# A two-layer hybrid decoder trunk: the down projection's second column half by seven products, and a convolution's lags split over two engines

## The chip, the cores and the metric

One core of one Trainium2 chip runs the whole program. The metric is the device time of one execution in microseconds (us). Engines are named as in the profile: PE is TensorE (matmuls), PEld its weight loads, DVE is VectorE, ACT is ScalarE, POOL is GpSimd, and SP is SyncE, which here only issues transfers.

## The reference

Two layers over 256 tokens of width 2048, in float32. Each layer is a mixer with a residual add, a gated feed-forward block with a convolution, and a gated per-layer embedding. Only the feed-forward block is touched:

```python
def causal_dwconv(x, w):                      # width 3, along the tokens
    width, s = w.shape[0], x.shape[1]
    xp = jnp.pad(x, ((0, 0), (width - 1, 0), (0, 0)))
    y = xp[:, 0:s] * w[0]
    for j in range(1, width):
        y = y + xp[:, j:j + s] * w[j]
    return y

def conv_ffn(hn, w_up, conv_w, conv_b, w_down):
    u = causal_dwconv(hn @ w_up, conv_w) + conv_b   # w_up: 2048 x 11264
    gate, up = jnp.split(u, 2, axis=-1)
    return (jax.nn.silu(gate) * up) @ w_down        # w_down: 5632 x 2048
...
h = h + conv_ffn(rmsnorm(h, ffn_norm), w_up, conv_w, conv_b, w_down)
```

## The kernel before

**Split precision.** A float32 operand is cut into a high part (`hi`, a cast on ScalarE, line 188) and a rest (`lo`, a difference on VectorE, line 189), in pieces of 128 x 1024. A product takes three matmuls: high by high, rest by high, high by rest. Four buffers for `hi` and four for `lo` (`WB`) set how far the casts run ahead of TensorE. Weights arrive in four raw buffers of 1 MiB (`RAWB`), loaded through SP's queue.

**The up projection.** `conv` handles 256 channels. `gemm_b` makes them in two units; a unit reads 1 MiB of weights, casts two pieces and issues 16 matmuls of 512 columns (line 267, both parts of the activations side by side) and 16 of 256 (line 272). `joined` adds the two halves of the PSUM result (lines 279, 280) and scales it (line 282). Then come the convolution (line 1072: one tap and the bias on ScalarE; line 1074: the two lags on VectorE), the gate (lines 1083, 1084) and `put_split`, which cuts the result into an activation tile (lines 482, 483). Two tiles of 128 channels of the feed-forward width (44 in all) take two such convolutions, one for the gate and one for the other half.

**The down projection.** `w_down` is worked through in groups of eight tiles, the first of four: (0,4), (4,12), ... (36,44). While one group is made by `up`, the group before it is multiplied by `down`, a unit of one between units of the other. A plain unit (`gemm_a`) takes four tiles by 512 columns for both token halves: 24 matmuls (lines 296, 297, 302).

**Seven products.** For the four groups in the middle, the first 1024 of the 2048 columns are done as a 2 x 2 block product with seven block products and not eight (`seven`). The left factors, sums of the activation blocks, are made by `Forms` (lines 381 to 389). The right factors are sums of weight blocks: a running total in two activation-sized buffers (`xg`), loaded by SP (`put`, line 408) and added to by transfers that POOL issues with an addition (`plus`, line 412), and fresh blocks in raw buffers (`fresh`). One product (`product`, lines 443, 444, 448) has 12 matmuls and casts two pieces. VectorE adds the results into `h` (lines 454 to 479); one sum of two weight blocks is made on VectorE (line 472). The other 1024 columns go by `plain` (line 1100).

**Order.** Each engine runs its queue in order. A scheduler of the framework orders the instructions of each engine when the program is built, from the order of the calls and their dependences. `SHARE` is 0.8: after each up unit 0.8 of a unit of `down` is due. `down` alternates one unit of `plain` with two of `seven`. The up projection runs two units (`LAG`) before the first of them. After the last group, `proj_add` does its down projection plainly (the tail) and feeds the next normalization (lines 316 to 338).

Of the kernel before, what the change touches and what calls it, by code (L numbers as in the profile page):

```python
# [16 lines left out]
AF = mybir.ActivationFunctionType  # L17
# [4 lines left out]
P = 128  # L22
# [11 lines left out]
UNIT = 3  # L34
LAG = 2
SHARE = 0.8
RATES = [1.7, 1.1, 1.1, 0.95, 2.8]
# [48 lines left out]
def trunk(ctx: ExitStack, tc: tile.TileContext, a: dict):  # L86
# [311 lines left out]
    class Quads:  # L398
# [15 lines left out]
        def begin(self):  # L414
            self.put(self.total, 0, 0)
            self.plus(0, 1)

# [8 lines left out]

    def seven(quads, tiles, forms, then):

        c, run_t, fresh, plus = quads.c, quads.total, quads.fresh, quads.plus

# [20 lines left out]
        h11, h12, h21, h22 = h[0][c], h[0][c + 1], h[1][c], h[1][c + 1]  # L451
        one = pb()
        yield from product(one, forms.left(0), run_t, True)
        V.tensor_sub(h22, h22, one)
        V.tensor_sub(h12, h12, one)
        plus(1, 1)
        acc = pb()
        yield from product(acc, x(0, 0), fresh(0, 0), True)
        V.tensor_add(h11, h11, acc)
        one = pb()  # L460
        yield from product(one, x(1, 0), fresh(1, 0), True)
        V.tensor_add(h11, h11, one)
        yield from product(acc, forms.left(1), run_t, False)
        V.tensor_sub(h12, h12, acc)
        plus(1, 0)
        one = pb()
        b22 = fresh(1, 1)
        yield from product(one, forms.left(3), b22, True)
        V.tensor_sub(h12, h12, one)
        t3 = fresh(0, 1)  # L470
        for q in range(2):
            V.tensor_add(t3[q], t3[q], b22[q])
        yield from product(acc, forms.left(2), t3, False)
        V.tensor_sub(h22, h22, acc)
        V.tensor_add(h21, h21, acc)
        one = pb()
        yield from product(one, x(1, 1), run_t, True)
        then()
        V.tensor_add(h21, h21, one)

# [575 lines left out]
    def ffn(l, nf, nxt, aside=None):  # L1056
# [9 lines left out]
        def conv(cb, j0):  # L1066
            ps = yield from gemm_b(w_up, cb, Xf)
            u = joined(ps, nf.bc)
            y = t2((P, 2, S))
            for j in range(2):  # L1070
                ct = j0 + j
                A.activation(y[:, j], u[:, j], AF.Identity, scale=fc(ct + 176), bias=fc(ct + 264))  # L1072
                for lag in range(1, 3):
                    V.scalar_tensor_tensor(y[:, j, lag:], u[:, j, : S - lag], fc(ct + (2 - lag) * 88), y[:, j, lag:], op0=ALU.mult, op1=ALU.add)  # L1074
            return y
# [15 lines left out]

        def down(g0, g1, tiles, forms, quads, then):
            r0, nk = g0 * P, g1 - g0

            def plain(cols):
                for c in cols:
                    ps = [pb() for _ in range(NH)]
                    yield from gemm_a(w_dn, r0, nk, c * 512, 512, tiles, ps)
                    for i in range(NH):
                        V.tensor_add(h[i][c], h[i][c], ps[i])  # L1100

            if forms is None:
                then()
                yield from plain(range(CG))
                return
            fast = seven(quads, tiles, forms, then)
            slow = plain(range(2, CG))
            going = True
            while going:
                going = False  # L1110
                for part in (slow, fast, fast):
                    for _ in range(UNIT):
                        if next(part, part) is not part:
                            going = True
                            yield

        groups = [(max(g - 4, 0), g + 4) for g in range(0, NFT, 8)]
        prev = None
        total = []

        def following(g0):
            if g0 + 8 < NFT:
                if not total:
                    total.extend(running())
                quads.append(Quads(w_dn, g0 * P, 0, total))
                quads[-1].begin()

        quads = []
        for g0, g1 in groups:
            forms = Forms() if 0 < g0 and g1 < NFT else None  # L1130
            cur = (g0, g1, [], forms)
            going = up(g0, g1, cur[2], forms)
            if prev is not None:
                behind_it = down(*prev, quads[-1] if quads else None, partial(following, g0))
                for _ in range(LAG * UNIT):
                    next(going)
                owed = 0.0
                for n, _ in enumerate(going, 1):
                    if n % UNIT:
                        continue  # L1140
                    owed += SHARE
                    if owed >= 1.0:
                        owed -= 1.0
                        for _ in range(UNIT):
                            next(behind_it, None)
                run(behind_it)
            else:
                run(going)
            if g0 == 4 and aside is not None:
                aside()  # L1150
            if g1 + 8 == NFT:
                pin.append(ple_input(l))
# [342 lines left out]
```

## Time and profile before

| | before |
|---|---|
| median of 3 runs | 2880.49 us (2878.83 to 2880.64) |
| profiled execution | 2880.58 us, span 2878.8 us |
| PE busy | 2860.8 us (99%) |
| DVE busy | 2060.9 us (72%) |
| ACT busy | 1537.8 us (53%) |
| transfers | 562.49 MB, mean 195 GB/s |

The span goes from the first to the last instruction of the one execution that the profiler recorded; its own time is 1.8 us longer. Busy times are unions per engine and can overlap between engines. The two feed-forward stages lie at about 500 to 1200 and 2100 to 2725 us of the span.

### The profile page before, as it was taken

How to read it: one execution, taken by the hardware profiler on the slowest of the kernel's cores; microseconds unless marked ns; L12 is line 12 of the kernel's file. 1: busy time of each engine (PE TensorE's matmuls, PEld its weight loads, DVE VectorE, ACT ScalarE, POOL GpSimd, SP SyncE). 2: the span in 40 equal slices, each digit the busy share in tenths (PEclk: the TensorE clock that was granted, in tenths of full speed). 3: DMA queues.
4: the chain of work that ended last, by engine and by line, in shares of the span. 5: the costliest groups of instructions: out<-in, count | busy, mean ns of one | idle time of the engine just before them, and what ended most of it. 6: DMA issues, size and time to landing. Idle time of an engine off the chain costs nothing.

```text
span 2878.8 us, 38652 instructions
## 1 busy us (share of the span) xinstructions
PE 2860.8 (99%) x15076; PEld 2464.2 (86%) x15076; DVE 2060.9 (72%) x2898; ACT 1537.8 (53%) x2185; POOL 121.8 (4%) x116
## 2 busy tenths in 40 slices
PE   9999999999999999999999999999999999999998
PEld 8899988888888888888888888888888888888887
DVE  7888867778878887656556565655668878788765
ACT  7666655555555555554444444344545555555554
POOL 0111100000000000000000000000000000000000
PEclk9999999999999999999999999999999999999999
DMA  7444445757878787555555555555575777877654
GB/s 236 135 132 131 138 161 194 221 189 203 249 206 235 233 232 225 171 183 192 179 185 186 191 181 182 186 179 189 186 222 185 220 232 223 238 220 223 212 185 145
DMA packets 410040, 562.49 MB, mean 195 GB/s; under 512 B 10752, under 2 KB 266880, under 8 KB 409856
## 3 DMA queue, kind: packets, MB, share of 16 engines
q1 hardware_dynamic: 393376, 530.05, 56.2%
q0 software_dynamic: 13056, 25.17, 5.3%
q10 hardware_dynamic: 3424, 4.79, 0.5%
q8 instruction: 118, 1.93, 0.3%
q14 instruction: 66, 0.54, 0.1%
HBM read 557.87 MB, written 2.10 MB: 195 GB/s over the span
## 4 chain that ended last, share of the span: by engine, by line
PE 98%; DVE 1%; ACT 0%; DMA 0%; issue 0%; POOL 0%; ACTq 0%; POOLq 0%; DVEq 0%
PE pa L267 30%; PE pa L272 16%; PE pa L297 10%; PE pa L296 10%; PE pa L302 10%; PE pb L297 3%; PE pb L296 3%; PE pb L302 3%; PE pb L444 2%; PE pb L443 2%; PE pb L448 2%; PE pb L739 2%; PE pb L316 1%; PE pa L936 1%; PE pb L745 0%; PE pb L1234 0%
## 5 line engine op out<-in xcount | busy, mean ns | idle before, releaser
L189 DVE TENSOR_TENSOR lo<-raw,hi 128x1024 fp32r<-128x1024 f32 (+3 forms) x1140 | 1197.9, 1075 | 555.8 <-ACT hi L188 498.8
L188 ACT CAST hi<-raw 128x1024 fp32r<-128x1024 f32 (+3 forms) x1140 | 1010.0, 931 | 955.5 <-PE pa L297 327.6
L267 PE MATMUL pa<-xg,hi 128*128 128x512 f32 x3840 | 925.9, 392 | 0.0
L267 PEld LDWEIGHTS pa<-xg,hi 128*128 128x128 f32 x3840 | 709.7, 188 | 140.6 <-DVE xg L321 0.3
L296 PE MATMUL pa<-hi,xg 128*128 128x512 f32 (+1 forms) x1348 | 522.8, 388 | 2.0 <-ACT hi L188 1.9
L297 PE MATMUL pa<-hi,xg 128*128 128x512 f32 (+1 forms) x1348 | 521.4, 387 | 0.3 <-DVE xg L321 0.2
L272 PEld LDWEIGHTS pa<-xg,lo 128*128 128x128 f32 x3840 | 490.3, 191 | 16.3
L272 PE MATMUL pa<-xg,lo 128*128 128x256 f32 x3840 | 502.0, 283 | 0.0
L302 PE MATMUL pa<-lo,xg 128*128 128x512 f32 (+1 forms) x1348 | 331.7, 386 | 0.0
L296 PEld LDWEIGHTS pa<-hi,xg 128*128 128x128 f32 x1348 | 253.9, 188 | 50.5 <-ACT hi L188 2.2
L297 PEld LDWEIGHTS pa<-hi,xg 128*128 128x128 f32 x1348 | 253.7, 188 | 49.4 <-DVE xg L321 0.8
L302 PEld LDWEIGHTS pa<-lo,xg 128*128 128x128 f32 x1348 | 250.1, 188 | 47.9
L1074 DVE SCALAR_TENSOR_TENSOR t<-t,fp,t 128x255 f32<-128x255 f32 (+1 forms) x352 | 154.0, 479 | 49.8 <-ACT t L1072 48.5
L297 PE MATMUL pb<-hi,xg 128*128 128x512 f32 x348 | 135.9, 391 | 0.0
L296 PE MATMUL pb<-hi,xg 128*128 128x512 f32 x348 | 135.8, 390 | 0.0
L279 ACT COPY t<-pa 128x512 f32<-128x512 f32 x128 | 75.1, 587 | 76.8 <-PE pa L272 67.6
L412 POOL DMA_DIRECT2D xg<-in_l_ffn_w_down_dram x48 | 57.9, 1206 | 1174.5 <-DVE t L1074 419.9
L1072 ACT ACTIVATE t<-t,fp 128x256 f32<-128x256 f32 x176 | 96.1, 593 | 13.4 <-DVE t L282 13.4
L157 POOL TENSOR_TENSOR small<-small,mhalf 128x1 f32<-128x1 f32 (+2 forms) x38 | 28.8, 757 | 1401.1 <-DVE small L1264 622.6
L280 DVE TENSOR_TENSOR t<-t,pa 128x512 f32<-128x512 f32 x128 | 87.1, 680 | 1.1 <-ACT t L279 1.1
L302 PE MATMUL pb<-lo,xg 128*128 128x512 f32 x348 | 86.5, 389 | 0.0
L321 DVE SCALAR_TENSOR_TENSOR xg<-pb,par,xg 128x256 fp32r<-128x256 f32 x136 | 60.0, 479 | 35.8 <-ACT xg L320 35.0
(280 smaller groups left out, 2233.8 us busy)
## 6 DMA issues: line engine op xcount, KB each, us to landing
raw<-in_l_ffn_w_up_dram SPq DMA_DIRECT2D x176, 1024.0 KB, 5.2
raw<-in_l_w_in_dram SPq DMA_DIRECT2D x128, 1024.0 KB, 5.1
raw<-in_l_ffn_w_down_dram SPq DMA_DIRECT2D x56, 1024.0 KB, 5.2
raw<-in_l_w_out_dram SPq DMA_DIRECT2D x44, 1024.0 KB, 5.1
raw<-in_l_ffn_w_down_dram SPq DMA_DIRECT2D x64, 512.0 KB, 4.9
raw<-in_l_ple_gate_dram SPq DMA_DIRECT2D x32, 1024.0 KB, 5.1
xg<-in_l_ffn_w_down_dram POOLq DMA_DIRECT2D x48, 512.0 KB, 6.8
xg<-in_l_ffn_w_down_dram SPq DMA_DIRECT2D x16, 512.0 KB, 4.6
```

The costliest lines, as they stand in the source:

```text
L188: last_cast[0] = A.copy(vo(hi)[:, c], vi(rk)[:, c])
L189: last_diff[0] = V.tensor_sub(vo(lo)[:, c], vi(rk)[:, c], vo(hi)[:, c].bitcast(F32))
L267: last_mm[0] = T.matmul(ps[:, j], wh, x2, start=first, stop=False)
L272: last_mm[0] = T.matmul(ps[:, j, :S], lo[k][:, j * P : (j + 1) * P], xr(tiles, c * 8 + k)[1], start=False, stop=c == 1 and k == 7)
L279: A.copy(u, ps[:, :, S:])
L280: V.tensor_add(u, u, ps[:, :, :S])
L296: T.matmul(o[i], xh, hi[k], start=begin and k0 + k == 0, stop=False)
L297: last_mm[0] = T.matmul(o[i], xw, hi[k], start=False, stop=False)
L302: last_mm[0] = T.matmul(o[i], xl(tiles, k0 + k, i)[0], lo[k], start=False, stop=end and k0 + k == nkb - 1)
L321: V.scalar_tensor_tensor(t[:, kk, 1], pk, g, t[:, kk, 0].bitcast(F32), op0=ALU.mult, op1=ALU.subtract)
L1072: A.activation(y[:, j], u[:, j], AF.Identity, scale=fc(ct + 176), bias=fc(ct + 264))
L1074: V.scalar_tensor_tensor(y[:, j, lag:], u[:, j, : S - lag], fc(ct + (2 - lag) * 88), y[:, j, lag:], op0=ALU.mult, op1=ALU.add)
```

## The change

The groups start at tile 0 and have eight tiles: (0,8), (8,16), ... (32,40), and the last has four, (40,44). `by_seven` says which column halves of a group go by seven products: both for the first four groups, the first half for (32,40). The last group is plain, as the tail. With both halves by seven, `down` has two `seven` one after the other and no plain part; the units due after each up unit follow from the count of units (1.0 there, 11/6 in the last group).

Within `seven` the order of the products changes. The running total starts as the block B11 alone (one load) and is used for the first product as it is; the block B12 is added afterwards. Before, B11 was loaded a second time, fresh. Products now add on in the same PSUM bank after VectorE has read it, so that seven additions into `h` are left of nine. At the end, `then` loads the total for the next half.

The two lags of the convolution were four operations on VectorE for 256 channels (multiply and add, 254 or 255 elements). They become four scaled copies on ScalarE (256 elements each) and two additions on VectorE over both channel blocks.

```diff
--- before.py
+++ after.py
@@ -33,7 +33,6 @@
 PSB = 4
 UNIT = 3
 LAG = 2
-SHARE = 0.8
 RATES = [1.7, 1.1, 1.1, 0.95, 2.8]
 D = 2048
 S = 256
@@ -413,7 +412,6 @@
 
         def begin(self):
             self.put(self.total, 0, 0)
-            self.plus(0, 1)
 
         def fresh(self, hh, e):
             raw = rawp.tile([P, 4, 512], F32, tag="raw", name=nm("raw"))
@@ -424,8 +422,9 @@
     def running():
         return [xtile().bitcast(F32).rearrange("p a b c -> p a (b c)") for _ in range(2)]
 
-    def seven(quads, tiles, forms, then):
-
+    def seven(ready, tiles, forms, then):
+
+        quads = ready.popleft()
         c, run_t, fresh, plus = quads.c, quads.total, quads.fresh, quads.plus
 
         def x(half, i):
@@ -449,34 +448,31 @@
             yield
 
         h11, h12, h21, h22 = h[0][c], h[0][c + 1], h[1][c], h[1][c + 1]
-        one = pb()
-        yield from product(one, forms.left(0), run_t, True)
-        V.tensor_sub(h22, h22, one)
-        V.tensor_sub(h12, h12, one)
-        plus(1, 1)
         acc = pb()
-        yield from product(acc, x(0, 0), fresh(0, 0), True)
+        yield from product(acc, x(0, 0), run_t, True)
         V.tensor_add(h11, h11, acc)
+        plus(0, 1)
         one = pb()
         yield from product(one, x(1, 0), fresh(1, 0), True)
         V.tensor_add(h11, h11, one)
+        two = pb()
+        yield from product(two, forms.left(0), run_t, True)
+        V.tensor_sub(h22, h22, two)
+        plus(1, 1)
+        b22 = fresh(1, 1)
+        yield from product(two, forms.left(3), b22, False)
+        V.tensor_sub(h12, h12, two)
+        t3 = fresh(0, 1)
+        for q in range(2):
+            V.tensor_add(t3[q], t3[q], b22[q])
         yield from product(acc, forms.left(1), run_t, False)
         V.tensor_sub(h12, h12, acc)
         plus(1, 0)
-        one = pb()
-        b22 = fresh(1, 1)
-        yield from product(one, forms.left(3), b22, True)
-        V.tensor_sub(h12, h12, one)
-        t3 = fresh(0, 1)
-        for q in range(2):
-            V.tensor_add(t3[q], t3[q], b22[q])
         yield from product(acc, forms.left(2), t3, False)
         V.tensor_sub(h22, h22, acc)
+        yield from product(acc, x(1, 1), run_t, False)
+        then()
         V.tensor_add(h21, h21, acc)
-        one = pb()
-        yield from product(one, x(1, 1), run_t, True)
-        then()
-        V.tensor_add(h21, h21, one)
 
     def put_split(t, k, n, src):
         A.copy(t[:, k : k + n, 0], src)
@@ -1070,8 +1066,11 @@
             for j in range(2):
                 ct = j0 + j
                 A.activation(y[:, j], u[:, j], AF.Identity, scale=fc(ct + 176), bias=fc(ct + 264))
-                for lag in range(1, 3):
-                    V.scalar_tensor_tensor(y[:, j, lag:], u[:, j, : S - lag], fc(ct + (2 - lag) * 88), y[:, j, lag:], op0=ALU.mult, op1=ALU.add)
+            for lag in range(1, 3):
+                z = t2((P, 2, S))
+                for j in range(2):
+                    A.activation(z[:, j], u[:, j], AF.Copy, scale=fc(j0 + j + (2 - lag) * 88))
+                V.tensor_add(y[:, :, lag:], y[:, :, lag:], z[:, :, : S - lag])
             return y
 
         def up(g0, g1, tiles, forms):
@@ -1089,66 +1088,68 @@
                         forms.add(*kept)
                         kept = []
 
-        def down(g0, g1, tiles, forms, quads, then):
-            r0, nk = g0 * P, g1 - g0
-
-            def plain(cols):
-                for c in cols:
-                    ps = [pb() for _ in range(NH)]
-                    yield from gemm_a(w_dn, r0, nk, c * 512, 512, tiles, ps)
-                    for i in range(NH):
-                        V.tensor_add(h[i][c], h[i][c], ps[i])
-
-            if forms is None:
-                then()
-                yield from plain(range(CG))
-                return
-            fast = seven(quads, tiles, forms, then)
-            slow = plain(range(2, CG))
+        def plain(g0, g1, tiles, cols):
+            for c in cols:
+                ps = [pb() for _ in range(NH)]
+                yield from gemm_a(w_dn, g0 * P, g1 - g0, c * 512, 512, tiles, ps)
+                for i in range(NH):
+                    V.tensor_add(h[i][c], h[i][c], ps[i])
+
+        groups = [(g, min(g + 8, NFT)) for g in range(0, NFT, 8)]
+        by_seven = {g0: [0, 2] if n < len(groups) - 2 else [0] for n, (g0, g1) in enumerate(groups[:-1])}
+        jobs = deque((g0, c) for g0, cols in by_seven.items() for c in cols)
+        ready = deque()
+        total = []
+
+        def following():
+            if not total:
+                total.extend(running())
+            if jobs:
+                g0, c = jobs.popleft()
+                ready.append(Quads(w_dn, g0 * P, c, total))
+                ready[-1].begin()
+
+        def down(g0, g1, tiles, forms):
+            fast = chain(*[seven(ready, tiles, forms, following) for _ in by_seven[g0]])
+            rest = [c for c in range(CG) if c - c % 2 not in by_seven[g0]]
+            slow = plain(g0, g1, tiles, rest)
+            parts = [slow, fast, fast] if rest else [fast]
             going = True
             while going:
                 going = False
-                for part in (slow, fast, fast):
+                for part in parts:
                     for _ in range(UNIT):
                         if next(part, part) is not part:
                             going = True
                             yield
 
-        groups = [(max(g - 4, 0), g + 4) for g in range(0, NFT, 8)]
         prev = None
-        total = []
-
-        def following(g0):
-            if g0 + 8 < NFT:
-                if not total:
-                    total.extend(running())
-                quads.append(Quads(w_dn, g0 * P, 0, total))
-                quads[-1].begin()
-
-        quads = []
-        for g0, g1 in groups:
-            forms = Forms() if 0 < g0 and g1 < NFT else None
+        for n, (g0, g1) in enumerate(groups):
+            forms = Forms() if g1 < NFT else None
             cur = (g0, g1, [], forms)
             going = up(g0, g1, cur[2], forms)
-            if prev is not None:
-                behind_it = down(*prev, quads[-1] if quads else None, partial(following, g0))
-                for _ in range(LAG * UNIT):
-                    next(going)
+            for _ in range(LAG * UNIT):
+                next(going)
+            if prev is None:
+                following()
+                run(going)
+            else:
+                behind_it = down(*prev)
+                share = sum(7 if c in by_seven[prev[0]] else 2 for c in range(0, CG, 2)) + 2 * (len(by_seven[prev[0]]) == 1)
+                share /= 2 * (g1 - g0) - LAG
                 owed = 0.0
-                for n, _ in enumerate(going, 1):
-                    if n % UNIT:
+                for m, _ in enumerate(going, 1):
+                    if m % UNIT:
                         continue
-                    owed += SHARE
-                    if owed >= 1.0:
+                    owed += share
+                    while owed >= 1.0:
                         owed -= 1.0
                         for _ in range(UNIT):
                             next(behind_it, None)
                 run(behind_it)
-            else:
-                run(going)
-            if g0 == 4 and aside is not None:
+            if n == 1 and aside is not None:
                 aside()
-            if g1 + 8 == NFT:
+            if n == len(groups) - 2:
                 pin.append(ple_input(l))
             prev = cur
         later(lambda: pin.append(ple_tiles(pin.pop())))
```

## Rows read from the trace of the kernel before

**Rows 1.** The page: busy us of each engine; the chain that ended last, by engine.

```profile
PE 2860.8 (99%) x15076; PEld 2464.2 (86%) x15076; DVE 2060.9 (72%) x2898; ACT 1537.8 (53%) x2185; POOL 121.8 (4%) x116
...
PE 98%; DVE 1%; ACT 0%; DMA 0%; issue 0%; POOL 0%; ACTq 0%; POOLq 0%; DVEq 0%
```

**Rows 2.** Windows: stretch, length, busy us (instructions) by engine, clock, DMA share, GB/s.

```profile
500.00:1200.00 700.00, 700.00 (x3734) 605.43 (x3733) 556.21 (x735) 392.51 (x496) 29.00 (x24) 1.00 0.72 218
2100.00:2725.00 625.00, 625.00 (x3349) 542.07 (x3348) 497.43 (x647) 349.82 (x430) 28.91 (x24) 1.00 0.73 220
890.55:1020.41 129.86, 129.86 (x694) 112.49 (x693) 105.46 (x138) 73.67 (x90) 7.22 (x6) 1.00 0.76 227
```

**Rows 3.** Timeline of PE in that group: start, us, line, operands, count.

```profile
903.23 3.82 PE L267 MATMUL pa<-xg,hi 128*128 128x512 f32 x16
...
906.88 2.08 PE L272 MATMUL pa<-xg,lo 128*128 128x256 f32 x16
...
908.79 3.82 PE L267 MATMUL pa<-xg,hi 128*128 128x512 f32 x16
...
919.93 0.40 PE L296 MATMUL pb<-hi,xg 128*128 128x512 f32 x1
...
925.39 3.79 PE L267 MATMUL pa<-xg,hi 128*128 128x512 f32 x16
...
930.93 0.40 PE L443 MATMUL pb<-hi,t 128*128 128x512 f32 x1
...
933.68 3.79 PE L267 MATMUL pa<-xg,hi 128*128 128x512 f32 x16
```

**Rows 4.** Groups by form, DVE, 890.55 to 1020.41: busy us, mean ns | idle before.

```profile
L189 DVE TENSOR_TENSOR lo<-raw,hi 128x1024 fp32r<-128x1024 f32 x48 | 57.9, 1220 | 14.9 <-ACT hi L188 14.0 <-PE pa L272 0.6 <-issue 0.3
...
L1074 DVE SCALAR_TENSOR_TENSOR t<-t,fp,t 128x255 f32<-128x255 f32 x16 | 7.3, 480 | 3.4 <-ACT t L1072 3.4
L1074 DVE SCALAR_TENSOR_TENSOR t<-t,fp,t 128x254 f32<-128x254 f32 x16 | 7.2, 479 | 0.1
L282 DVE TENSOR_TENSOR t<-t,rbc 128x512 f32<-128x512 f32 x8 | 5.5, 685 | 0.0
...
L1100 DVE TENSOR_TENSOR t<-t,pb 128x512 f32<-128x512 f32 x4 | 2.7, 684 | 5.0 <-PE pb L302 5.0
L472 DVE TENSOR_TENSOR raw<-raw,raw 128x1024 f32<-128x1024 f32 x2 | 2.5, 1226 | 0.1
```

**Rows 5.** Groups by form, ACT, the same stretch.

```profile
L188 ACT CAST hi<-raw 128x1024 fp32r<-128x1024 f32 x48 | 48.4, 1048 | 37.6 <-PE pa L267 19.4 <-issue 9.6 <-PE pb L297 6.0
L1072 ACT ACTIVATE t<-t,fp 128x256 f32<-128x256 f32 x16 | 8.7, 594 | 1.5 <-DVE t L282 1.5
```

**Rows 6.** Line 320, a copy with a scale: ns min/median/max, first and last start.

```profile
L320 ACT ACTIVATE xg<-pb,par x136: 454/467/515, 7.7 to 2775.0; 128x256 fp32r<-128x256 f32 x136
```

**Rows 7.** DMA queues, 890.55 to 1020.41: packets, MB, share of 16 engines.

```profile
q1 hardware_dynamic: 21464, 26.21, 61.2%
q0 software_dynamic: 1632, 3.15, 14.5%
```

**Rows 8.** Timeline around one addition to the running total.

```profile
922.87 1.05 ACT L188 CAST hi<-xg 128x1024 fp32r<-128x1024 f32 x1 [2.16 <-PE pb L297]
...
927.30 1.22 DVE L189 TENSOR_TENSOR lo<-xg,hi 128x1024 fp32r<-128x1024 f32 x1
927.54 2.50 POOL L412 DMA_DIRECT2D xg<-in_l_ffn_w_down_dram  x2 [29.22 <-DVE t L1074]
```

**Rows 9.** The page, DMA issues: count, KB each, median us to landing.

```profile
xg<-in_l_ffn_w_down_dram POOLq DMA_DIRECT2D x48, 512.0 KB, 6.8
xg<-in_l_ffn_w_down_dram SPq DMA_DIRECT2D x16, 512.0 KB, 4.6
```

**Rows 10.** Timeline of ACT at the end of a layer's last up unit.

```profile
1154.87 0.59 ACT L279 COPY t<-pa 128x512 f32<-128x512 f32 x1 [0.82 <-PE pa L272]
...
1163.09 0.63 ACT L482 CAST xg<-t 128x512 fp32r<-128x512 f32 x1 [0.24 <-DVE t L1084]
```

## The prediction

> **What bounds the kernel now.** I read the page first: TensorE is busy for nearly the whole span [rows 1]. That alone proves little, since matmuls overlap in the trace, so the windows over the two feed-forward stages come next. The change lies wholly in these 1,325 us, and there TensorE is busy for 700.00 of 700.00 and 625.00 of 625.00 us, with the clock at 1.00 [rows 2], its upper level of 2.4 GHz. The chain of waits agrees: nothing but matmul lines, one behind the other. So a wait of another engine costs nothing today, and a matmul that goes is worth its distance to the next one.
>
> Third comes the timeline of one group, for that distance. A unit of the up projection starts its 512-column matmuls at 903.23, its 256-column ones at 906.88, and the next unit starts at 908.79: 5.56 us. A plain unit of the down projection (24 matmuls) runs from 919.93 to 925.39: 5.46 us. A product of the seven (12 matmuls) from 930.93 to 933.68: 2.75 us [rows 3]. Check: a group of eight tiles now takes 16 up units, 7 products and 4 plain units, 88.96 + 19.25 + 21.84 = 130.05 us; its period in the trace, from one reload of the running total at 890.55 to the next, is 129.86.
>
> Fourth, the other resources of that group: VectorE is busy 105.46 us of 129.86 (81%), ScalarE 73.67 (57%), the DMA engines 76% [rows 2]. These are the covers that the change spends.
>
> **The change part by part.**
>
> *Fewer matmuls.* Today four groups of a layer do one column half by seven products and one plainly; the rest is plain. Afterwards the five full groups do nine of ten halves by seven. A half costs 4 plain units, 21.84 us, or 7 products, 19.25: 2.59 saved. Five halves more in each of two layers: 10 x 2.59 = 25.9 us. Counted by matmuls it is 12 fewer per half, 120 x 0.228 (3.65/16, [rows 3]) = 27.4; I take 25.9, which contains the joints between units, and 27.4 as the outer bound.
>
> *VectorE.* In a group whose down projection is all seven (four per layer), the 32 lag operations go: 7.3 + 7.2 us. In their place stand 16 additions of 510 or 508 elements. Nearest row: the 512-element addition with both operands in SBUF, 5.5 us for 8, so 11.0. The second half makes 14 casts where the plain one made 8; six more differences at 57.9/48 = 1.21 are 7.2. The sum for one product (b22 into t3) comes twice, +2.5. Additions into h: 7 + 7 instead of 9 + 4, +0.7 [rows 4]. Sum: 105.5 - 14.5 + 11.0 + 7.2 + 2.5 + 0.7 = 112.4 us. The group itself shrinks to 16 x 5.56 + 14 x 2.75 = 127.5. So VectorE goes from 81% to 88%: hidden, with 15 us of slack instead of 24.
>
> *ScalarE.* Per group 32 scaled copies of 256 elements come new. None like them, SBUF to SBUF with a column as scale, is in the trace: below is the copy with such a scale out of PSUM, 0.467 [rows 6], above the activation with scale and bias, 0.594 [rows 5]. That is 15 to 19 us; I take 16, nearer to the copy, since only the scale is read. Six more casts at 48.4/48 = 1.01 add 6. Total 73.7 + 16 + 6 = 96 us of 127.5, 75%: hidden in sum.
>
> *DMA.* Per group the up weights stay 16 MiB. A seven's half drops from 8 to 7 MiB (B11 is now used from the running total and not loaded again), but the plain half of 4 becomes 7; three of each seven are additions into SBUF, on POOL's queue. Today SP's queue takes 61.2% of 129.86 us for 26.21 MB, 3.03 us a MB, and POOL's 14.5% for 3.15 MB, 5.98 [rows 7]. Afterwards 25.2 x 3.03 + 6.3 x 5.98 = 76 + 38 = 114 us, 89% of 127.5. Hidden, but the second cover that becomes thin.
>
> *The running total.* It is cast for products 1, 3, 5 and 7, and an addition lands in between. Products 1 and 3 are now two up units and one product apart, 16.6 us start to start. In the trace, from the first cast of such a product (922.87) the last difference starts at 927.30 and ends at 928.5, and POOL issues two additions from 927.54 [rows 8]. They land after 6.8 us [rows 9]. The first half is thus there 11.5 us and the second about 13 us after the first cast. 3.6 us are left, so I price it at zero; the casts' lead over TensorE (922.87 against 930.93, 8 us) covers it, too.
>
> The reload from the seventh product to the first of the second half is tighter, because only one up unit lies between: 8.3 us start to start. The last difference ends 5.6 us after the first cast, and a 512 KB load takes 4.6 [rows 9]: 10.2 to 11, so 2 to 2.7 us late, behind a lead of 8. Zero again, and 2.7 at most without the lead. The loads queued behind this one on SP are for the units after it; four raw buffers, no longer used for B11, hold them early. Between groups three up units lie in between, 16.7 us.
>
> *PSUM.* Products now add on in a bank that VectorE must read first (3 to 4, 5 to 6, 6 to 7). An up unit of 5.56 us stands between for an addition of 0.68 [rows 4]. Zero; in the short last group pairs can touch, which is at most a few times 0.7 us.
>
> *The regrouping.* Groups now start at tile 0, so the first up group runs alone for 16 units instead of 8, and the last holds 4 tiles. The tail after the last up unit still waits for the last activated tile. Today the chain from reading the last PSUM (1154.87) to the cast of that tile (1163.09 + 0.63) takes 8.9 us [rows 10]. What covers it is one product, one plain unit and four matmuls, 2.75 + 5.46 + 0.9 = 9.1. The tail now needs that tile in its first plain unit; ahead of it stand the last two units of the group before, one plain and one product: 9.1 again. The chain grows by four scaled copies, 4 x 0.47 less what the VectorE saves there (4 x 0.48 - 2 x 0.69 = 0.5): +1.4 us. So about 1.2 us stand open per layer; with wake-ups I take 1.5, 3.0 in all. Bounds: 0, and 2 x 3 if nothing overlaps.
>
> **Sum.** The profiled execution took 2880.58 us (span 2878.8); the median of the runs is 2880.49, so it stands for it. 2880.58 - 25.9 + 3.0 = 2857.7, say **2858**.
>
> **Rivals.**
> *Late reload* (B): the lead of the casts does not survive at VectorE's 88% and DMA's 89%, and each of the 8 reloads inside a group stalls TensorE by 2.7 us: 2854.7 + 21.6 = 2876, a null. For it: three resources lose slack at once. Against it: the lead of 8 us, and not a single wait of TensorE at 76% to 81%.
>
> *VectorE becomes the bound* (C, the other side): its queue is in order, and an addition into h that waits for its product holds the casts behind it. Today the plain additions wait 5.0 us per group, 2.5 for each that waits [rows 4]; those of the seven show none. From 130.7 us per group (112.4 + 18.3 of waits, 1.3 for each of 14 products) the whole gain is gone (25.9/8 + 127.5). At 1.5 each it is 133.4: 8 x 5.9 = 47 over the 2854.7, about 2902. Against it: an up unit stands between product and next product, so the sum is usually done when VectorE comes to it.
>
> *ScalarE in front of the casts* (D): the four copies of a convolution stand ahead of the hi casts of the next unit, 4 x 0.47 = 1.9 us. They are free while the lead is over 1.9. If it is not, each of the 88 convolutions shows them: 2854.7 + 167 = 3022. Against it: 25% of free time on that engine. The Trainium skill, "ScalarE: Activation LUTs", section "Rules for kernel authors", speaks against the edit, too: it sends multiplications and additions to VectorE. By that rule the lag work would stay where it was, at 14.5 us of VectorE per group, and the edit would lose time. The rows give VectorE a relief of only 3.5 us for 16 of ScalarE, so the rule is right about the exchange rate; it decides the time only if ScalarE has no slack, and 75% says that it has. The same page's section "What ACT_TABLE_LOAD costs" would give an estimate of 0.49 us for such a copy (186 + 93 + 256 x 0.833 ns), 15.8 us per group, and the same sum; no run here shows that copy yet.
>
> **How the numbers follow.** About 0.2% of the time, 5.8 us, is what a measurement of this kernel can tell from no change. My forecast has 0.69 and its own range is 2853 to 2866. B has 0.13 (of it 0.05 faster, 0.06 within 0.2%, 0.02 slower), C 0.13, D 0.05. That makes 0.74 faster, 0.06 the same, 0.20 slower. The range takes in the forecast and B: from 2852 (27.4 saved without a stall, and a microsecond of spread) to 2880; C and D, 0.18, are left out.
>
> **What would show it.** Right: a steady group lasts about 127.5 us, the PSUM matmuls of the seven are 9 x 84 per layer, TensorE stays at 100% in the windows of both stages, VectorE near 88%, ScalarE near 75%, DMA near 89%; the new copy takes 0.47 to 0.5 us and the joint addition 0.69. A gap of 1 to 2 us on TensorE stands at the first tail unit of each layer. Wrong: gaps on TensorE after each seventh product, with casts that wait for the running total (B); groups over 130 us in which VectorE waits for PSUM while casts are ready (C); or ScalarE at over 90% with TensorE waiting for hi (D).

## The result, and the profile after

The changed kernel takes 2854.49 us (median of 4 runs, 2853.68 to 2856.61) against 2880.46 (4 runs): a ratio of 0.9912, 95% interval 0.9895 to 0.9929. That is 26.0 us less. The profiled execution took 2854.34 us, span 2852.6. The forecast was 2858.

The page of the changed kernel, busy us of each engine, answers to [rows 1]:

```profile
PE 2833.9 (99%) x14956; PEld 2440.1 (86%) x14956; DVE 2137.8 (75%) x2840; ACT 1735.0 (61%) x2605; POOL 194.9 (7%) x176
```

TensorE lost 120 matmuls and 26.9 us of work (2860.8 to 2833.9). Its idle time, span less busy, went from 18.0 to 18.7 us. So the whole gain is work taken from the engine that sets the pace, and only 0.7 us of it were given back.

The windows of the changed kernel over the two stages and one steady group (from one reload of the total to the same reload a group later), answer to [rows 2]:

```profile
500.00:1180.00 680.00, 679.27 (x3631) 587.34 (x3630) 585.26 (x692) 481.94 (x684) 65.59 (x54) 1.00 0.83 237
2080.00:2700.00 620.00, 620.00 (x3324) 537.48 (x3323) 537.40 (x625) 442.77 (x625) 65.53 (x54) 1.00 0.85 240
...
817.09:944.23 127.14, 127.14 (x682) 110.24 (x681) 112.27 (x131) 91.86 (x128) 14.55 (x12) 1.00 0.90 250
```

A steady group takes 127.14 us where it took 129.86, with TensorE busy all the time. Three covers got thin together (a cover is an engine whose work is hidden behind TensorE's): VectorE 112.27 us (88%), ScalarE 91.86 (72%), DMA 90%.

Groups by form of the changed kernel in that group, VectorE and then ScalarE, answer to [rows 4, 5]:

```profile
L188 DVE TENSOR_TENSOR lo<-raw,hi 128x1024 fp32r<-128x1024 f32 x44 | 52.9, 1219 | 9.9 <-ACT hi L187 6.8 <-issue 1.8 <-PE pa L271 0.9
...
L1073 DVE TENSOR_TENSOR t<-t,t 128x508 f32<-128x508 f32 x8 | 5.5, 688 | 0.7
...
L1073 DVE TENSOR_TENSOR t<-t,t 128x510 f32<-128x510 f32 x8 | 5.4, 680 | 0.0
...
L467 DVE TENSOR_TENSOR raw<-raw,raw 128x1024 f32<-128x1024 f32 x4 | 4.9, 1223 | 3.2 <-DMA raw<-in_l_ffn_w_down_dram 3.1
```

```profile
L187 ACT CAST hi<-xg 128x1024 fp32r<-128x1024 f32 x16 | 16.2, 1050 | 3.7 <-PE pb L443 3.1 <-DMA xg<-in_l_ffn_w_down_dram 0.6
L1072 ACT ACTIVATE t<-t,fp 128x256 f32<-128x256 f32 x32 | 13.6, 495 | 0.0
```

The joint additions take 10.9 us per group, and the copies 0.495 us each, 13.6 together because neighbours overlap. The two DMA queues in the group, answering to [rows 7]:

```profile
q1 hardware_dynamic: 21142, 25.32, 59.8%
q0 software_dynamic: 3264, 6.29, 29.4%
```

Transfers into the running total take longer to land than before, from the page (answering to [rows 9]). ScalarE's casts wait for some of them now, which they never did before; this row is from the list of waits (us in total, times, longest):

```profile
xg<-in_l_ffn_w_down_dram POOLq DMA_DIRECT2D x108, 512.0 KB, 7.1
...
xg<-in_l_ffn_w_down_dram SPq DMA_DIRECT2D x36, 512.0 KB, 6.8
```

```profile
ACT hi L187 <- DMA xg<-in_l_ffn_w_down_dram: 11.8, 13, 1.7
```

By the timeline all 13 waits stand at the eight reloads inside a group; no cast waits for an addition.

Timelines of TensorE and ScalarE at the first tail unit of layer 0 (in brackets the idle time before, and what ended it):

```profile
1156.57 0.40 PE L295 MATMUL pb<-hi,xg 128*128 128x512 f32 x1
1156.77 0.59 ACT L278 COPY t<-pa 128x512 f32<-128x512 f32 x1 [0.82 <-PE pa L271]
...
1164.75 0.39 PE L295 MATMUL pa<-hi,xg 128*128 128x512 f32 x1
...
1166.28 0.62 ACT L478 CAST xg<-t 128x512 fp32r<-128x512 f32 x1 [0.28 <-DVE t L1083]
1166.34 0.39 PE L296 MATMUL pa<-hi,xg 128*128 128x512 f32 x1
1166.95 0.73 PE L295 MATMUL pa<-hi,xg 128*128 128x512 f32 x2 [0.22 <-ACT xg L478]
1168.04 0.50 PE L296 MATMUL pa<-hi,xg 128*128 128x512 f32 x1 [0.35 <-DVE xg L479]
```

### The profile page after: what moved, and what is told of

The parts are those of the page before. It is cut to its first block, busy times and chain, and to the rows that moved or that the text cites. A ratio compares the mean times of both kernels' runs of the same rounds, so it can differ in the third digit from the quotient of the medians.

```text
span 2852.6 us, 39163 instructions
## 1 busy us (share of the span) xinstructions
PE 2833.9 (99%) x14956; PEld 2440.1 (86%) x14956; DVE 2137.8 (75%) x2840; ACT 1735.0 (61%) x2605; POOL 194.9 (7%) x176
## 4 chain that ended last, share of the span: by engine, by line
PE 97%; DVE 1%; DMA 0%; ACT 0%; issue 0%; POOL 0%; ACTq 0%; POOLq 0%; DVEq 0%
PE pa L266 30%; PE pa L271 16%; PE pa L301 10%; PE pa L296 10%; PE pa L295 10%; PE pb L443 4%; PE pb L442 4%; PE pb L447 4%; PE pb L735 2%; PE pb L315 1%; PE pb L296 1%; PE pb L295 1%; PE pb L301 1%; PE pa L932 1%; PE pb L741 0%; DVE lo L188 0%
## 5 line engine op out<-in xcount | busy, mean ns | idle before, releaser
L188 DVE TENSOR_TENSOR lo<-raw,hi 128x1024 fp32r<-128x1024 f32 (+3 forms) x1104 | 1151.2, 1070 | 508.1 <-ACT hi L187 404.7
L187 ACT CAST hi<-raw 128x1024 fp32r<-128x1024 f32 (+3 forms) x1104 | 968.7, 926 | 737.6 <-PE pa L296 329.7
L295 PE MATMUL pa<-hi,xg 128*128 128x512 f32 (+1 forms) x1284 | 497.4, 388 | 2.5 <-ACT hi L187 1.9
L296 PE MATMUL pa<-hi,xg 128*128 128x512 f32 (+1 forms) x1284 | 495.6, 386 | 1.0 <-DVE xg L479 0.7
L295 PEld LDWEIGHTS pa<-hi,xg 128*128 128x128 f32 x1284 | 241.0, 188 | 49.2 <-ACT hi L187 2.2
L296 PEld LDWEIGHTS pa<-hi,xg 128*128 128x128 f32 x1284 | 241.2, 188 | 47.6 <-DVE xg L479 1.6
L411 POOL DMA_DIRECT2D xg<-in_l_ffn_w_down_dram x108 | 131.1, 1232 | 1188.4 <-DVE lo L188 1085.0
L188 DVE TENSOR_TENSOR lo<-xg,hi 128x1024 fp32r<-128x1024 f32 x144 | 172.5, 1218 | 9.3 <-ACT hi L187 9.2
L187 ACT CAST hi<-xg 128x1024 fp32r<-128x1024 f32 x144 | 145.6, 1049 | 31.7 <-PE pb L443 15.5
L1072 ACT ACTIVATE t<-t,fp 128x256 f32<-128x256 f32 x352 | 149.1, 495 | 0.0
L1068 ACT ACTIVATE t<-t,fp 128x256 f32<-128x256 f32 x176 | 96.2, 594 | 60.2 <-DVE t L281 60.2
L1073 DVE TENSOR_TENSOR t<-t,t 128x510 f32<-128x510 f32 (+1 forms) x176 | 120.4, 684 | 8.3 <-ACT t L1072 0.5
L443 PE MATMUL pb<-hi,t 128*128 128x512 f32 x288 | 113.0, 393 | 0.0
L442 PE MATMUL pb<-hi,t 128*128 128x512 f32 x288 | 113.0, 392 | 0.0
```

The source lines that it names most:

```text
L187: last_cast[0] = A.copy(vo(hi)[:, c], vi(rk)[:, c])
L188: last_diff[0] = V.tensor_sub(vo(lo)[:, c], vi(rk)[:, c], vo(hi)[:, c].bitcast(F32))
L295: T.matmul(o[i], xh, hi[k], start=begin and k0 + k == 0, stop=False)
L296: last_mm[0] = T.matmul(o[i], xw, hi[k], start=False, stop=False)
L411: G.dma_start(self.total[q], self.blocks[q, hh, e], accum_op=ALU.add)
L442: T.matmul(o, l[0], hi[k], start=start and q + k == 0, stop=False, skip_group_check=True)
```

## The experiments

The forecast was right in time. Right could still mean that errors cancelled, so the experiments ask which parts of the change matter and how near each rival was. Each kernel was timed together with the kernel before, whose median lay between 2879.02 and 2880.28 us; a difference from the changed kernel (2854.49) is good to a microsecond or two.

**One part alone, the lags.** The kernel before, with only this edit:

```diff
-                for lag in range(1, 3):
-                    V.scalar_tensor_tensor(y[:, j, lag:], u[:, j, : S - lag], fc(...), y[:, j, lag:], ...)
+            for lag in range(1, 3):
+                z = t2((P, 2, S))
+                for j in range(2):
+                    A.activation(z[:, j], u[:, j], AF.Copy, scale=fc(...))
+                V.tensor_add(y[:, :, lag:], y[:, :, lag:], z[:, :, : S - lag])
```

> The kernel before, with only the convolution's lags moved (scaled copies on ScalarE, joint additions on VectorE). If TensorE alone sets the pace of the feed-forward stages and the other engines are covers, nothing changes: 2880.5 us, within 2 us, while VectorE's busy time in a steady group falls from 105.5 to about 102 us and ScalarE's rises from 73.7 to about 88. If VectorE's load was already part of the time, this kernel is faster by several us. If copies in front of the casts hold TensorE up, it is slower; only the tail may show up to 1.5 us per layer.

Measured: 2879.17 us against 2879.02, ratio 1.0001 (0.9992 to 1.0009). No change. VectorE's busy time fell as expected (102.64 us, about 102 expected), ScalarE's rose a little less (85.82, about 88 expected). Windows of this kernel, one group:

```profile
889.31:1019.17 129.86, 129.86 (x694) 112.49 (x693) 102.64 (x122) 85.82 (x122) 7.22 (x6) 1.00 0.76 227
```

**The other part alone.** The changed kernel with the lags back on VectorE (the edit above, reversed).

> The changed kernel with the lags left on VectorE as before. VectorE gets 112.3 + 3.5 = 116 us of 127 per steady group, 91%. If the lead of the casts covers that, the time is that of the changed kernel, 2854.5, or up to 3 us better at the tail, where the chain is shorter: 2852 to 2856. If VectorE is close to being the bound and its relief is what made the change work, each steady group is held up by 1 us and more: 2863 or above.

Measured: 2853.7 us, ratio 0.9913 (0.99 to 0.9927), where the full change has 0.9912. Windows of this kernel, one group:

```profile
817.09:944.23 127.14, 127.14 (x682) 110.24 (x681) 114.39 (x148) 79.93 (x96) 14.48 (x12) 1.00 0.90 248
```

The group has the same 127.14 us with VectorE at 90%. The lag edit brings nothing here; all of the gain is the down projection's. Nor do the copies open the gap at the tail: without them TensorE waits there, too, 0.7 us per layer (waits of TensorE: us in total, times, longest).

```profile
PE pa L296 <- DVE xg L479: 1.4, 2, 0.7
```

The kernel with the lags alone has no wait for that tile, so the gap comes with the rest of the change, where the tail needs the tile earlier.

**Fewer halves.**

```diff
-    by_seven = {g0: [0, 2] if n < len(groups) - 2 else [0] ...
+    by_seven = {g0: [0] ...
```

> The changed kernel, but only the first column half of each of the five full groups by seven products, the second plainly. Compared with the kernel before this is one half more per layer by seven, and all the rest of the change (groups from tile 0, order of the products, lags). If the time is the distance between matmuls, it is 2880.5 - 2 x 2.6 = 2875.3, and 20.7 us (8 x 2.59) slower than the changed kernel. If other parts of the change (fewer loads, fewer additions into h, shorter tail) bring a part of the gain, it is clearly below 2873.

Measured: 2876.01 us against 2879.02, ratio 0.999 (0.9981 to 0.9999). Two halves more than before give 3.0 us (0.3 to 5.5 by the interval, 5.2 expected), and the eight that are missing cost 22 against the changed kernel by the two ratios (0.999 and 0.9912; 20.7 expected). TensorE's busy time says it more sharply: 2855.2 us, which is 5.6 under the kernel before with 24 matmuls fewer, and 21.3 over the changed kernel with 96 more. The gain goes by the count of halves.

**VectorE loaded further.** Two kernels, with 2 and with 4 idle additions per convolution:

```diff
                 V.tensor_add(y[:, :, lag:], y[:, :, lag:], z[:, :, : S - lag])
+            for _ in range(2):                  # 4 in the second kernel
+                V.tensor_add(u, u, u)
```

> The changed kernel with two more additions of 512 elements on VectorE per convolution (on a tile that is no longer read). Per steady group 16 x 0.61 = 9.8 us more: 112.3 + 9.8 = 122 us of 127, 96%. If VectorE's waits are nearly all backpressure from being ahead, the group stays near 127 us and the time is 2855 to 2862. If waits of 1.3 us per product cannot be hidden (rival C), the group takes 122 + 18 = 140 us: 8 x 13 = +104 us.

> The changed kernel with four more additions per convolution on VectorE: 19.5 us per steady group, 131.8 us against TensorE's 127. VectorE must now be the bound; how far the group is over 131.8 shows the waits that VectorE cannot hide. With none the group takes 132 us, and with 8 groups and some us in the other stretches the time is 2854.5 + 8 x 4.7 = 2892 to 2900; with 18 us of waits per group it is near 3040.

Measured: 2854.54 us (ratio 0.9911, 0.9898 to 0.9925) with two, 2920.33 (1.0141, 1.0127 to 1.0155) with four. A group's windows with two, then with four:

```profile
817.09:944.23 127.14, 127.14 (x682) 110.27 (x681) 120.21 (x147) 92.17 (x128) 14.58 (x12) 1.00 0.89 249
```

```profile
707.02:840.25 133.23, 128.96 (x681) 109.88 (x681) 129.93 (x163) 92.40 (x128) 14.57 (x12) 1.00 0.85 237
840.25:972.71 132.46, 128.98 (x682) 109.89 (x681) 129.95 (x163) 93.47 (x130) 14.55 (x12) 1.00 0.86 239
```

At 120.21 us of 127.14 (95%) VectorE still costs nothing. With four its busy time is 129.9 us (131.8 were expected), and the groups, from one reload to the next, take 133.2 and 132.5: 2.5 to 3.3 us of waits that it cannot hide, not the 18 that rival C needed. The total is higher than the 2892 to 2900 expected. Between the same reloads of the two traces the six later groups of the layers lose 5.3 to 8.1 us each, 39 of the 69 by which the span grew; 17 are lost before the first of these reloads in layer 0, and 14 between the last one of layer 0 and the first of layer 1.

**ScalarE loaded further.**

```diff
                     A.activation(z[:, j], u[:, j], AF.Copy, scale=fc(...))
+                    A.activation(z[:, j], u[:, j], AF.Copy, scale=fc(...))
```

> The changed kernel with each scaled copy done twice on ScalarE. Per steady group that is 32 more copies, 13.6 us: ScalarE goes from 92 to 105.5 us of 127, 83%. If ScalarE is a cover with slack, steady groups stay at 127 us and only the tail's chain grows by 1.7 us per layer: 2855 to 2860. If the copies stand in front of the casts that TensorE needs (rival D), each of 88 convolutions shows 1.7 us more: about +150 us.

Measured: 2866.68 us (ratio 0.9952, 0.9938 to 0.9965), 12 over the changed kernel: more than the 5 expected, far from 150. In layer 0 TensorE waits 3.88 us, where the changed kernel waits 0.73 (windows of this kernel):

```profile
500.00:1180.00 680.00, 676.12 (x3611) 583.19 (x3610) 582.26 (x687) 543.68 (x852) 65.78 (x54) 1.00 0.83 236
1150.00:1190.00 40.00, 38.14 (x182) 30.50 (x181) 30.38 (x41) 26.51 (x45) 0.00 (x0) 1.00 0.66 202
```

Half of that, 1.86, stands at the tail, where the chain grew. Another 1.6 lie between 600 and 680 us, in the first group with products beside it: one wait for a difference and one for a cast, so the copies do come in the way of casts in places. In the next groups, from 680 to 1040 us, there is none. Over the profiled execution TensorE is idle 7.6 us longer than in the changed kernel (2863.0 - 2836.7 against 18.7) and busy 2.8 us longer.

**The reload later.**

```diff
             self.put(self.total, 0, 0)
+            self.put(self.total, 0, 0)
```

> The changed kernel, in which the running total's first block is loaded twice in a row before each half (the same bytes; the second load waits for the first), so that it is ready about 5 to 7 us later, and SP's queue is held up as long. Nothing is left out. If the lead of the casts (some 8 us, less the 2 to 2.7 by which the reload inside a group is late already) covers it, little shows: 2854.5 to 2860. If the reload inside a group stands open already (rival B), each of the 8 such reloads adds its 5 to 7 us: 2895 to 2910.

Measured: 2865.44 us (ratio 0.9949, 0.9937 to 0.9962), 11 over the changed kernel. A reload inside a group in the changed kernel, timelines of ScalarE, VectorE and SP's queue (last column: idle before, and what ended it):

```profile
756.41 2.01 ACT L187 CAST hi<-xg 128x1024 fp32r<-128x1024 f32 x2 [0.34 <-PE pb L443]
...
759.13 2.35 DVE L188 TENSOR_TENSOR lo<-xg,hi 128x1024 fp32r<-128x1024 f32 x2
...
760.38 1.50 SPq L407 DMA_DIRECT2D xg<-in_l_ffn_w_down_dram  x2
...
765.48 1.05 ACT L187 CAST hi<-xg 128x1024 fp32r<-128x1024 f32 x1 [1.21 <-DMA xg<-in_l_ffn_w_down_dram]
```

and with the double load the second piece of the new total there, and all waits of TensorE for such casts:

```profile
775.24 1.05 ACT L187 CAST hi<-xg 128x1024 fp32r<-128x1024 f32 x1 [2.36 <-DMA xg<-in_l_ffn_w_down_dram]
...
PE pb L443 <- ACT hi L187: 6.6, 8, 1.7
```

In the changed kernel the cast of the new total already waits 1.21 us for the load, 9.1 us after the first cast of the seventh product; TensorE starts on it at 771.85, so 6.4 us of lead are left and nothing shows. With the double load the second piece is cast 16.3 us after the first cast of the seventh product, where it was 10.3, and TensorE waits for it, 0.82 us here and 6.6 over the eight reloads inside a group. The time lies between the two expectations (2854.5 to 2860, 2895 to 2910): of a delay of 6.0 us most is covered, but not all. The rest of the 11 us, and whether SP's busier queue has a part in it, stays open; TensorE's busy time is 4.7 us longer (2838.6 against 2833.9).

**The tenth half.**

```diff
-    by_seven = {g0: [0, 2] if n < len(groups) - 2 else [0] ...
+    by_seven = {g0: [0, 2] ...
```

> The changed kernel with the tenth half, too, by seven products: both halves of tiles 32 to 40, worked off in the six slots of the last short group, so that two or three products follow one another without an up unit between them. By matmul distance alone it saves 2 x 2.59 = 5.2 us: 2849.3. If products that touch wait for VectorE to read the shared bank and for the running total (7 us to land, while two products last 5.5), a part is given back: with 5 us and more of such waits per layer it is slower than the changed kernel, 2856 to 2870.

Measured: 2882.96 us (ratio 1.0016, 1.0007 to 1.0025): fewer matmuls, and 28.5 us slower than the changed kernel, more than the 2856 to 2870 expected. Timelines of ScalarE, VectorE and TensorE of this kernel in the short last group:

```profile
1168.94 1.04 ACT L187 CAST hi<-xg 128x1024 fp32r<-128x1024 f32 x1 [5.01 <-DMA xg<-in_l_ffn_w_down_dram]
...
1170.01 1.23 DVE L188 TENSOR_TENSOR lo<-xg,hi 128x1024 fp32r<-128x1024 f32 x1 [4.12 <-ACT hi L187]
1171.16 0.68 DVE L469 TENSOR_TENSOR t<-t,pb 128x512 f32<-128x512 f32 x1
...
1171.98 0.76 PE L442 MATMUL pb<-hi,t 128*128 128x512 f32 x1 [5.93 <-DVE t L469]
```

Read from below: TensorE waits 5.93 us for a subtraction into `h` of 0.68 us. That subtraction stood in VectorE's queue behind a difference, that one waited for its cast, and the cast for the addition into the running total to land. The product whose result it reads had long ended. The row names VectorE; the cause is a transfer.

Two more kernels, both with the tenth half, tell the transfer from the shared bank. In the first, products 4, 6 and 7 get banks of their own (and h gets eleven additions); in the second, the transfers that add go.

```diff
-        yield from product(acc, forms.left(2), t3, False)
-        V.tensor_sub(h22, h22, acc)
+        six = pb()
+        yield from product(six, forms.left(2), t3, True)
+        V.tensor_sub(h22, h22, six)
+        V.tensor_add(h21, h21, six)
...
```

```diff
         def plus(self, hh, e):
             for q in range(2):
-                G.dma_start(self.total[q], self.blocks[q, hh, e], accum_op=ALU.add)
+                pass
```

> The kernel with ten halves by seven, in which no product adds on in a PSUM bank that VectorE has just read: products 4, 6 and 7 get banks of their own, and VectorE makes eleven additions into h per half, not seven. If the 28 us that the tenth half cost come from products that wait for VectorE to read the shared bank, most of them go: 2850 to 2860. If they come from the running total, which lands too late where two products touch, the waits stay and move to the casts: 2878 to 2888.

> The kernel with ten halves by seven, without the three transfers per half that add to the running total: the weight blocks B12, B22 and B21 are left out of it, so the output is not the reference's; matmuls, casts and additions on VectorE stay. If the additions to the running total are what the tenth half waits for, nearly all of its 28 us go and the 5.2 us of fewer matmuls appear: 2849 to 2855. If PSUM, VectorE or the mere crowding of products is the cause, it stays at 2865 or above.

Measured: 2909.9 us with banks of their own (ratio 1.0104, 1.0089 to 1.0119), 2855.7 without the transfers (0.9917, 0.99 to 0.9933). Waits of TensorE in both, total us, times, longest:

```profile
PE pb L442 <- ACT hi L187: 21.4, 10, 3.1
```

```profile
PE pb L442 <- DVE t L469: 5.7, 4, 1.7
...
PE pb L442 <- DVE t L472: 1.2, 2, 0.6
```

Without the transfers 27 us of the loss are gone, so they are the cause (by the rows above through their landing; the DMA time that they take goes with them). The 5.2 us of fewer matmuls do show in TensorE's busy time (2828.7 against 2833.9), but 6.9 us of waits for the shared bank eat them. With banks of their own the waits move to the casts, as the second expectation said, and the kernel gets slower still (2909.9, where 2878 to 2888 were expected); whether by the four more additions or because the four buffers are taken up sooner, is not told apart.

**The old order of the seven products** in the changed kernel: first the product that needs B11 + B12, so that a load and an addition stand before it. This kernel also loads B11 a second time and makes nine additions into `h`, as the kernel before did.

```diff
             self.put(self.total, 0, 0)
+            self.plus(0, 1)
...
-        yield from product(acc, x(0, 0), run_t, True)
+        yield from product(one, forms.left(0), run_t, True)
+        V.tensor_sub(h22, h22, one)
+        V.tensor_sub(h12, h12, one)
+        plus(1, 1)
+        acc = pb()
+        yield from product(acc, x(0, 0), fresh(0, 0), True)
...
```

> The changed kernel with the body of the seven products as it was: first the factor that needs B11 + B12 (one load, then one addition, before the first product), B11 loaded again for the second product, nine additions into h, no shared banks after a read. Within a group the total is then ready some 18 us after the first cast of the seventh product (5.6 to the last difference, 4.6 to 6.8 for the load, 7 for the addition), 8.3 us are there and a lead of about 8 us: 2 us and more open at each of the 8 places, and DMA goes from 89 to about 94%. So 2870 to 2890, if the running total's chain is the nearest limit. If it is not, and only TensorE counts, 2854.5 as now.

Measured: 2924.76 us (ratio 1.0156, 1.0141 to 1.0171), 70 over the changed kernel and 46 over the kernel before, far above the 2870 to 2890 expected. The reload inside a group, timelines of SP's queue, POOL, ScalarE and TensorE of this kernel, then all its waits of TensorE for such casts, and its windows there:

```profile
771.77 2.15 SPq L407 DMA_DIRECT2D xg<-in_l_ffn_w_down_dram  x2
...
776.64 1.20 POOL L411 DMA_DIRECT2D xg<-in_l_ffn_w_down_dram  x1 [28.14 <-DMA xg<-in_l_ffn_w_down_dram]
...
786.09 1.04 ACT L187 CAST hi<-xg 128x1024 fp32r<-128x1024 f32 x1 [6.72 <-DMA xg<-in_l_ffn_w_down_dram]
...
787.18 0.80 PE L443 MATMUL pb<-hi,t 128*128 128x512 f32 x1 [4.37 <-ACT hi L187]
...
790.11 0.79 PE L443 MATMUL pb<-hi,t 128*128 128x512 f32 x1 [0.85 <-ACT hi L187]
...
PE pb L443 <- ACT hi L187: 44.1, 16, 5.5
```

```profile
780.00:788.00 8.00, 3.63 (x22) 3.17 (x22) 1.08 (x2) 1.56 (x2) 0.00 (x0) 0.95 1.04 235
788.00:796.00 8.00, 7.15 (x21) 5.19 (x21) 6.88 (x9) 6.39 (x9) 2.41 (x2) 0.63 0.70 108
```

The first addition goes out when the load has landed, at 776.64, and the cast comes at 786.09: 14.3 us after the load was issued, where the changed kernel has 5.1 (760.38 to 765.48). The 16 waits stand two by two at the eight reloads inside a group. What the second load of B11 and the two more additions add to this is not told apart.

**The nine halves without the additions to the total** (the edit of the second kernel above, on the changed kernel).

> The changed kernel without the additions to the running total (B12, B22 and B21 are left out of it, so the output is not the reference's). The DMA share of a steady group falls from 90 to about 60%. If these transfers are hidden in the changed kernel, it stays at 2854.5 within 2 us. If part of the gain is already lost to a late total (rival B in part), it is faster by that part.

Measured: 2854.79 us (ratio 0.9913, 0.9899 to 0.9928), as the changed kernel. The transfers, 29.4% of the DMA engines' time in a group, are wholly hidden there.

## Why the prediction was right

*Fewer matmuls.* Forecast 25.9, bound 27.4; TensorE's busy time fell by 26.9 and a group by 2.72 us. The size is right, and the kernel with fewer halves agrees. The unit times, read off one stretch, made the forecast 1 us small.

*VectorE.* Forecast 112.4 us per group, measured 112.27. The slack that it left was real: 95% still costs nothing, and past 100% the groups follow VectorE's work within 2.5 to 3.3 us. Rival C is refuted in its mechanism, waits of 1.3 us per product; VectorE sets the pace only where its plain sum passes TensorE's.

*ScalarE.* Forecast 96, measured 91.86. The six more casts add 6.3 us (79.93 with the lags on VectorE, against 73.67), as forecast; the copies add 11.9 (91.86 against 79.93), not 16, since they overlap one another (13.6 us for 32 in the rows) and other work of the engine. Rival D falls: doubling the copies costs 12 us, not 150, though a few casts do come late by it. By the rule of the Trainium skill, "ScalarE: Activation LUTs", section "Rules for kernel authors", the lag work belonged on VectorE; the trace agrees on the exchange (with the lags alone, VectorE goes from 105.46 to 102.64 us and ScalarE from 73.67 to 85.82), and the kernel that follows it, with the lags on VectorE, has the same time. The estimate of 0.49 us for the copy, from the Trainium skill, "ScalarE: Activation LUTs", section "What ACT_TABLE_LOAD costs", met 0.495 in the rows.

*DMA.* Forecast 89%, measured 90%; hidden, as the kernel without the additions to the total shows.

*The running total.* Forecast zero, found zero, with a little more margin than forecast. At the eight reloads inside a group the load's first half takes 4.4 to 5.4 us from issue to cast (5.1 in the rows above), where 4.6 was assumed; the page's median of 6.8 counts the loads between groups, too, for which no cast waits. But the load is issued earlier: the prediction let it wait for the last difference, 5.6 us after the first cast of the seventh product, while each half is loaded when its own difference has ended, 4.0 us after that cast (756.41 to 760.38). So the new total's first cast comes 8.3 to 9.3 us after it, not 10.2 to 11, and TensorE starts on it 6.1 to 7.1 us later. The chain is still the nearest limit that the experiments found, nearer than VectorE: the double load, the tenth half and the old order lengthen it, or set its steps closer together, and cost 11, 28.5 and 70 us. So rival B named a real mechanism that this kernel does not reach. The forecast counted the new order as one load less; what the old order shows is that it is worth more, most likely because the first product needs one transfer and not two.

*The tail.* Forecast 1.5 us open per layer; TensorE waits 0.22 us for the cast of the last tile and 0.35 for its rest, 0.57 in each layer. The chain was sized rightly: 10.1 us from reading the last PSUM (1156.77) to the end of the cast (1166.28 + 0.62), 10.3 forecast. What covers it was too small in the forecast: eight matmuls of the tail's first unit stand before the tile (1164.75 to 1166.34), not four, so TensorE has 10.2 us of work of its own there (1156.57 to 1166.73), not 9.1. The term was right in place and sign and too large by 1.9 us in all. With the 1 us of the first term this is nearly all of the 3.2 between 2857.7 and 2854.5.

## What to carry to other kernels

Where one engine is busy without a gap, a change is worth the work that it takes from that engine, as long as each cover still holds. Price the covers one by one: here VectorE, whose queue runs ahead, held at 95% of the group and not at 102%. Look for the limit in chains that go through memory (read, transfer, read again), too, and not only in the busiest cover: here an order of products that lengthens such a chain cost 70 us, while a queue at 95% cost none. When a wait is put down to a short operation, ask what stood before it in the same in-order queue.

## What was not expected of the hardware

A late total costs twice. With the old order of the products TensorE is idle 65.5 us (2924.4 less 2858.9), 46.8 more than in the changed kernel; but the same 14,956 matmuls are also busy 25.0 us longer. The windows above show why at one of these places: after a stretch with 4.4 of 8 us idle, the granted clock of the next 8 us is 0.63, between its levels of 1.2 and 2.4 GHz, though TensorE is busy for 7.15 of them. The sum, 71.8, is the difference of the spans. A gap of 0.57 us, as in the tail, left the clock at 1.00.
